# Second mixture of experts with a written-out order on TensorE, and S5 states split by real and imaginary part over partition halves

## The chip, the cores and the metric

The kernel runs on one core of one Trainium2 chip. The time is the device time of one execution in microseconds (us); lower is better. The core's engines work side by side: PE (TensorE: matmuls; PEld is its weight load), DVE (VectorE), ACT (ScalarE), POOL (GpSimd), and SP, which here issues the DMA transfers. Each takes its instructions in a fixed order and waits where an operand is late.

## The reference

Two layers over 256 latent and 256 context tokens of width 1024. A layer runs four token mixers (windowed attention, a state-space scan, global attention, S5), merges them, and then a mixture of 32 experts, two per token. The first layer works on all 512 tokens, the second on the 256 latent ones. The parts that matter here:

```python
def s5_mixer(...):
    for direction in range(2):
        a_bar, b_bar = s5_discretise(...)
        s_l, _ = s5_scan(einsum('blgs,gns->blgn', ul, b_bar), a_bar, fin_c, rev)
        y_l = y_l + real(einsum('blgn,gsn->blgs', s_l, c_cplx))
def expert_dispatch(h, expert_idx, gate_w, w_gate, w_up, w_down):
    ...
    def expert_block(args):
        xb, e = args
        return (silu(xb @ w_gate[e]) * (xb @ w_up[e])) @ w_down[e]
    y = lax.map(expert_block, (x_blocks, block_expert))
    return zeros_like(h).at[slot_tok].add(y * slot_w[:, None])
```

S5 states are complex: a real and an imaginary part of 64 states for each of 32 channel groups. An expert has three weight matrices, gate and up of 1024x512 and down of 512x1024, 2 MB each in float32.

## The kernel before, in words

The program is one Python function per stage; a framework keeps the tiles and semaphores, and its scheduler puts each engine's instructions into an order by a simulated timeline (line 1972). `tc.issue_after(x)` pins what is written inside it behind instruction x on the same engine; without it the order on an engine is the scheduler's.

**The second mixture** (layer 1, `l == 1`) has 256 tokens in two tiles (`nt` = 2) and goes through all 32 experts. The weights of an expert come as six loads of 1 MB (`load`, L1655, tile `mraw`; gate, up, down in halves), all issued by SP in program order into a ring of 16 slots; a slot comes free when the matmuls that read it are done. For an expert e, with the tile names that the profile prints:

- `front1` (L1753): `sl`, a one-hot matrix of 128 tokens by 128 slots for each token tile (two comparisons on DVE, L1757); `slb`, its first 64 slots in bf16 (L1759); 48 bf16 matmuls that gather the expert's tokens into `px` (L1764), copied by ACT into `xgt`; two transposes of `sl` into `pst` (L1770) and two products of `sl` with the router weights that give one weight per slot in a column of `pst` (L1772); DVE copies `slt` (L1774) and `wcol` (L1776) out of it. The one-hot side of expert e is made while e-1 is worked on (`nxt`).
- `product` (L1687): gate and up, 16 matmuls each (L1694), into the two halves of `pgu`. Each is two matmul records in the profile.
- `swiglu` (L1668): `th` by tanh on ACT (L1670), then two steps on DVE (printed as L84).
- `down` (L1697): two transposes of `th` into `pat` (L1701), a copy `at` on ACT, eight products into `pd` (L1707).
- `expert1` (L1779): `yg` = `pd` x `wcol` x gate (two on DVE, L84), split into `yh` (ACT) and `yl` (DVE); eight products `po` (L1800) scatter them back, four for each token tile, and DVE adds each into `acc` (L1806, printed as L78).

Where PE takes up each of these pieces is the scheduler's choice. The first mixture (layer 0, `front0`, `expert0`) uses the same `product`, `swiglu` and `down`, with gathers and scatters by DMA.

**S5** (L785 to L873) works through four blocks q of eight channel groups in each layer. Per block it loads the tables `gt`, `W`, `R`, `Q` (1 MB, L806) and `M`; for both directions d it makes `pE` on PE, runs the scan on DVE, and writes the states to `SB` (L853 to L856). `SB` holds for each d, part r (real, imaginary) and a (4 pairs of groups) a block-diagonal matrix of 128 x 128: group h in rows and columns 64h to 64h+63, zero elsewhere (cleared once, L793). The outputs `pY` come from `M` (L860, weights of 64 columns for one group h) and from `SB` (L863, weights of 128 columns for both groups, one product per d and r).

## Time and profile before

| | |
|---|---|
| median of 3 runs | 2624.61 us (2623.95 to 2629.16) |
| the profiled execution | 2621.41 us |
| its span, first to last instruction | 2619.6 us |
| granted TensorE clock, mean | 0.934 |
| PE busy | 2246.3 us, 86% |
| DVE, ACT, POOL busy | 53%, 27%, 27% |
| second mixture, first to last `swiglu` | 2099.8 to 2591.0 us |
| S5 output products L863, layer 0 and layer 1 | 378.2 to 528.0 and 1753.0 to 1834.6 us |

The time of an execution is its span and some 2 us around it. A busy PE is not a PE at its peak: matmuls are pipelined, so the time that a piece of PE work takes is best read from the start of one row to the start of the next. The profile's names leave buffer numbers out, and its "x32" counts records, two for a float32 matmul and one for a bf16 matmul.

### The profile page before, as it was taken

To read this page: it belongs to the slowest core of one execution; us is meant where nothing else is said; L and a number is where in the kernel's file an instruction comes from. 1 tells how busy PE (TensorE), PEld (TensorE's weight loads), DVE (VectorE), ACT (ScalarE), POOL (GpSimd) and SP (SyncE) were. 2 spreads that over 40 slices of the span, in tenths; PEclk is the share of its full clock that TensorE was granted. 3 is DMA by queue.
4 is the path that set the end of the run, shared out by engine and by line. 5 is a ranking of instruction groups with operands and counts; after the bars stand their busy time and mean duration, and the time that the engine had idled before them with its cause. 6 is when DMAs were issued, how large, how long until landed. Compare 5 with 4: busy or idle time off the path is not lost. (4 is left out here: it accounts for less than half of the span.)

```text
span 2619.6 us, 41026 instructions
## 1 busy us (share of the span) xinstructions
PE 2246.3 (86%) x16006; PEld 1579.7 (60%) x16006; DVE 1379.4 (53%) x2755; ACT 695.9 (27%) x1344; POOL 716.4 (27%) x686
## 2 busy tenths in 40 slices
PE   5898987799996979988888749989888699999996
PEld 3677866577654755544444338878767566755553
DVE  7846888956753852000000286558587744443334
ACT  2334422145561201111111123533465211111110
POOL 8988787743120031111111032001132100000000
PEclk8999998899997979999999869999898799999998
DMA  6643476575765779999999955488656699999991
GB/s 244 183 137 122 136 198 206 167 247 182 238 195 159 253 271 372 415 409 415 412 410 411 373 175 154 147 251 266 227 175 178 264 364 421 422 423 403 369 387 71
DMA packets 287317, 710.67 MB, mean 271 GB/s; under 512 B 39886, under 2 KB 199038, under 8 KB 228240
## 3 DMA queue, kind: packets, MB, share of 16 engines
q1 hardware_dynamic: 280400, 694.72, 73.0%
q0 software_dynamic: 5280, 8.05, 1.0%
q10 hardware_dynamic: 1440, 5.24, 0.5%
q8 instruction: 128, 2.10, 0.3%
q14 instruction: 69, 0.57, 0.1%
HBM read 645.82 MB, written 71.37 MB: 274 GB/s over the span
## 5 line engine op out<-in xcount | busy, mean ns | idle before, releaser
L1694 PE MATMUL pgu<-mraw,xgt 128*64 128x256 f32 x4224 | 515.2, 386 | 29.1 <-DMA mraw<-in_moe_w_up_dram 28.0
L1694 PEld LDWEIGHTS pgu<-mraw,xgt 128*64 128x64 f32 x4224 | 314.1, 138 | 213.6 <-DMA mraw<-in_moe_w_up_dram 58.4
L84 DVE SCALAR_TENSOR_TENSOR th<-th,pgu 128x256 f32<-128x256 f32 x132 | 55.5, 420 | 498.6 <-ACT th L1670 496.5
L1707 PE MATMUL pd<-mraw,at 128*64 128x512 f32 x1056 | 258.8, 605 | 38.9 <-DMA mraw<-in_moe_w_down_dram 36.8
L507 PE MATMUL pfm<-hhi,hi 128*128 128x256 f32 (+1 forms) x832 | 283.0, 344 | 5.3 <-ACT hi L93 4.6
L508 PE MATMUL pfm<-hlo,hi 128*128 128x256 f32 (+1 forms) x832 | 283.7, 343 | 2.1 <-DVE hlo L78 2.0
L509 PE MATMUL pfm<-hhi,lo 128*128 128x256 f32 (+1 forms) x832 | 280.9, 342 | 4.0 <-DVE lo L78 3.7
L78 DVE TENSOR_TENSOR lo<-raw,hi 128x1024 fp32r<-128x1024 f32 (+1 forms) x147 | 205.5, 1399 | 93.6 <-ACT hi L93 89.2
L128 POOL TENSOR_TENSOR bnrs<-bnrs,mhalf 128x1 f32<-128x1 f32 x26 | 28.9, 1116 | 723.3 <-DVE bnrs L88 723.3
L93 ACT ACTIVATE hi<-raw 128x1024 fp32r<-128x1024 f32 (+1 forms) x160 | 169.2, 1059 | 204.2 <-PE pfm L508 124.7
L1707 PEld LDWEIGHTS pd<-mraw,at 128*64 128x64 f32 x1056 | 80.7, 137 | 164.3 <-issue 108.4
L507 PEld LDWEIGHTS pfm<-hhi,hi 128*128 128x128 f32 x832 | 158.4, 192 | 32.8 <-ACT hi L93 6.0
L509 PEld LDWEIGHTS pfm<-hhi,lo 128*128 128x128 f32 x832 | 157.8, 191 | 24.6 <-DVE lo L78 4.6
L508 PEld LDWEIGHTS pfm<-hlo,hi 128*128 128x128 f32 x832 | 158.9, 191 | 19.7 <-DVE hlo L78 2.9
L84 DVE SCALAR_TENSOR_TENSOR yg<-pd,wcol,g 64x512 f32<-64x512 f32 x64 | 48.0, 750 | 148.0 <-PE pd L1707 135.0
L1745 POOL DMA_INDIRECT yb_d<-ye,idx x30 | 29.9, 998 | 294.2 <-ACT ye L93 266.8
L507 PE MATMUL pm<-yh,hi 128*128 128x512 f32 (+1 forms) x256 | 90.6, 368 | 21.3 <-ACT yh L93 11.9
L78 DVE TENSOR_TENSOR acc<-acc,po 128x512 f32<-128x512 f32 x124 | 80.6, 684 | 51.9 <-PE po L1800 51.3
L508 PE MATMUL pm<-yl,hi 128*128 128x512 f32 (+1 forms) x256 | 92.3, 362 | 3.4 <-DVE yl L78 3.4
L1670 ACT ACTIVATE th<-pgu 128x256 f32<-128x256 f32 x66 | 25.3, 383 | 261.4 <-PE pgu L1694 261.4
L507 PE MATMUL ptm<-hi,hhi 128*128 128x256 f32 x320 | 92.4, 289 | 0.0
L508 PE MATMUL ptm<-lo,hhi 128*128 128x256 f32 x320 | 91.3, 286 | 0.0
(508 smaller groups left out, 4470.0 us busy)
## 6 DMA issues: line engine op xcount, KB each, us to landing
mraw<-in_moe_w_gate_dram SPq DMA_DIRECT2D x132, 1024.0 KB
mraw<-in_moe_w_up_dram SPq DMA_DIRECT2D x132, 1024.0 KB
mraw<-in_moe_w_down_dram SPq DMA_DIRECT2D x132, 1024.0 KB
raw<-in_w_in_dram SPq DMA_DIRECT2D x116, 512.0 KB
modr<-in_mod_w_dram SPq DMA_DIRECT2D x40, 1024.0 KB
modw<-in_mod_w_dram SPq DMA_DIRECT2D x8, 1024.0 KB
gt_d<-gt SPq DMA_DIRECT2D x16, 512.0 KB
q_d<-Q SPq DMA_DIRECT2D x32, 256.0 KB
```

Source lines behind the costliest of these rows:

```text
L78: V.tensor_tensor(o, a, b, op=op)
L84: V.scalar_tensor_tensor(o, a, s, b, op0=op0, op1=op1)
L93: S.activation(o, a, AF.Copy, scale=scale)
L128: G.tensor_tensor(o, a, b, op=OP.pow)
L507: T.matmul(p, ahi, bhi, start=first, stop=False)
L508: T.matmul(p, ahi, blo, start=False, stop=False)
L509: T.matmul(p, alo, bhi, start=False, stop=last)
L1670: S.activation(th, pg, AF.Tanh, scale=0.5)
L1694: T.matmul(p[64 * cb:64 * cb + 64, 256 * i:256 * i + 256], xt[:, kt], raw[:, k, 256 * cb:256 * cb + 256], start=(kt == 0), stop=(kt == KT ...
L1707: T.matmul(p[64 * nh:64 * nh + 64], at[:, j, 64 * cb:64 * cb + 64], raws[cb][:, j, nh], start=(k == 0), stop=(k == 3))
L1745: sc_ = G.indirect_dma_start(out=yb_d.rearrange("r (n c) -> (r n) c", n=2), out_offset=bass.IndirectOffsetOnAxis(ap=i, axis=0), in_=y, in_ ...
```

## The change

**The second mixture** gets a loop of its own, `experts1`, and its PE work is pinned piece behind piece. `in_order()` opens `issue_after` behind the last instruction kept in `behind`; it does nothing in layer 0, where `behind` stays empty. For expert e PE now takes: the gather of e+1 (`px`), the transposes `pst` of e+1, the scatter of expert e-2 for token tile 1, up of e, gate of e+1, the transposes `pat` of e, the scatter of expert e-1 for token tile 0, down of e. The loads follow this order: up of e, gate of e+1, down of e. `slb` is compared into bf16 directly; `slw`, in place of `sl`, is the comparison times the router weight; `slt` is the transposed `slw` compared with zero; `wcol` is its row sum on DVE, and the products of L1772 are gone. `slt` has four buffers. `route_over` (the list of overfull experts) is written at expert 3 instead of 2.

**S5**: `SB` keeps the real part in partitions 0 to 63 and the imaginary part in 64 to 127, for each d, h and a a matrix of 128 x 64 with no zeros. The products of L863 become one per d and h with 64 weight columns into the half of `pY` for h; their count is the same. `Q` is read by two transfers of 64 partitions each.

```diff
@@ -789,7 +789,8 @@
-            SB = s1.tile([128, 2, 2, 4, 128], F32, name="SB")
+            SB = s1.tile([128, 2, 2, 4, 64], F32, name="SB")
             V.memset(SB, 0.0)
...
@@ -803,7 +804,8 @@
                     Q = sq.tile([128, 2, 2, 4, 128], F32, tag="Q", name="Ql", bufs=1)
-                    dma(Q, q_d[l, q])
+                    for r in range(2):
+                        dma(Q[64 * r:64 * r + 64], q_d[l, q].rearrange("(h s) d r a x -> r s d h a x", h=2)[r])
...
@@ -846,7 +848,7 @@
                         for h in range(2):
                             hp = slice(64 * h, 64 * h + 64)
                             for r in range(2):
-                                o0 = SB[hp, d, r, :, 64 * h:64 * h + 64]
+                                o0 = SB[64 * r:64 * r + 64, d, h]
                                 i1, i2 = (m1[hp, 0], m2[hp, 1]) if r == 0 else (m1[hp, 1], m2[hp, 0])
...
@@ -859,9 +861,8 @@
                         for h in range(2):
                             T.matmul(py[64 * h:64 * h + 64, a], U[:, grp(a, h)], M[:, 2 * a + h], start=True, stop=False)
                         for d in range(2):
-                            for r in range(2):
-                                T.matmul(py[:, a], SB[:, d, r, a], Q[:, d, r, a], start=False,
-                                         stop=(d == 1 and r == 1))
+                            for h in range(2):
+                                T.matmul(py[64 * h:64 * h + 64, a], SB[:, d, h, a], Q[:, d, h, a], start=False, stop=(d == 1))
...
@@ -1684,6 +1685,17 @@
+        behind = [None]
+
+        @contextmanager
+        def in_order():
+            if behind[0] is None:
+                yield
+            else:
+                with tc.issue_after(behind[0].ins):
+                    yield
+
         def product(p, i, e, xt):
 
...
-                        T.matmul(p[64 * cb:64 * cb + 64, 256 * i:256 * i + 256], xt[:, kt],
-                                 raw[:, k, 256 * cb:256 * cb + 256], start=(kt == 0), stop=(kt == KT - 1))
-
-        def down(p, e, a):
+                        o = T.matmul(p[64 * cb:64 * cb + 64, 256 * i:256 * i + 256], xt[:, kt],
+                                     raw[:, k, 256 * cb:256 * cb + 256], start=(kt == 0), stop=(kt == KT - 1))
+            return o
+
+        def down(p, e, a, between=None):
             at = wk.tile([128, 2, 128], F32, tag="at", name="at2")
             pt = pb("pat")
-            for j in range(2):
-                T.transpose(pt[:, 128 * j:128 * j + 128], a.rearrange("q (p j) -> q j p", j=2)[:, j], ident)
+            with in_order():
+                for j in range(2):
+                    o = T.transpose(pt[:, 128 * j:128 * j + 128], a.rearrange("q (p j) -> q j p", j=2)[:, j], ident)
             copyS(at.rearrange("p a b -> p (a b)"), pt[:, :256])
+            if l:
+                behind[0] = o
+            if between:
+                between()
             raws = [load(rows_of(2, e, 256 * cb, 256)).rearrange("p (j n) c -> p j n c", j=2) for cb in range(2)]
-            for k in range(4):
-                cb, j = divmod(k, 2)
-                for nh in range(2):
-                    T.matmul(p[64 * nh:64 * nh + 64], at[:, j, 64 * cb:64 * cb + 64], raws[cb][:, j, nh],
-                             start=(k == 0), stop=(k == 3))
+            with in_order():
+                for k in range(4):
+                    cb, j = divmod(k, 2)
+                    for nh in range(2):
+                        o = T.matmul(p[64 * nh:64 * nh + 64], at[:, j, 64 * cb:64 * cb + 64], raws[cb][:, j, nh],
+                                     start=(k == 0), stop=(k == 3))
+            if l:
+                behind[0] = o
 
...
         def front1(e):
 
-            sl = wk.tile([128, nt, 128], F32, tag="sl", name="sl")
+            slb = wk.tile([128, nt, 64], BF16, tag="slb", name="slb")
+            slw = wk.tile([128, nt, 128], F32, tag="sl", name="slw")
             for t in range(nt):
-                ts(sl[:, t], slots[:, 1], rt["posx"][:, t, e:e + 1], None, OP.is_equal)
-            slb = wk.tile([128, nt, 64], BF16, tag="slb", name="slb")
-            V.tensor_copy(slb, sl[:, :, :64])
+                ts(slb[:, t], slots[:, 1, :64], rt["posx"][:, t, e:e + 1], None, OP.is_equal)
+            for t in range(nt):
+                ts(slw[:, t], slots[:, 1], rt["posx"][:, t, e:e + 1], rt["wx"][:, t, e:e + 1], OP.is_equal, OP.mult)
             px = pb("px")
-            for kt in range(KT):
+            pst = pb("pst")
+            with in_order():
+                for kt in range(KT):
+                    for t in range(nt):
+                        for i in range(3):
+                            T.matmul(px[:, 64 * kt:64 * kt + 64], rt["h2"][t][i][:, 128 * kt:128 * kt + 128], slb[:, t],
+                                     start=(t == 0 and i == 0), stop=(t == nt - 1 and i == 2))
                 for t in range(nt):
-                    for i in range(3):
-                        T.matmul(px[:, 64 * kt:64 * kt + 64], rt["h2"][t][i][:, 128 * kt:128 * kt + 128], slb[:, t],
-                                 start=(t == 0 and i == 0), stop=(t == nt - 1 and i == 2))
+                    behind[0] = T.transpose(pst[:, 128 * t:128 * t + 128], slw[:, t], ident)
             xt = wk.tile([128, KT, 64], F32, tag="xt", name="xgt")
             copyS(xt.rearrange("p a x -> p (a x)"), px)
-            pst = pb("pst")
-            for t in range(nt):
-                T.transpose(pst[:, 128 * t:128 * t + 128], sl[:, t], ident)
-            for t in range(nt):
-                T.matmul(pst[:, 256:257], sl[:, t], rt["wx"][:, t, e:e + 1], start=(t == 0), stop=(t == nt - 1))
-            slt = wk.tile([128, nt, 128], F32R, tag="slt", name="slt")
-            V.tensor_copy(slt.rearrange("p a x -> p (a x)"), pst[:, :128 * nt])
+
+            slt = wk.tile([128, nt, 128], F32R, tag="slt", name="slt", bufs=4)
+            ts(slt.rearrange("p a x -> p (a x)"), pst[:, :128 * nt], 0.0, None, OP.is_gt)
             wcol = wk.tile([128, 1], F32, tag="wcol", name="wcol")
-            V.tensor_copy(wcol, pst[:, 256:257])
+            V.tensor_reduce(wcol, pst[:, :128 * nt], axis=AXL.X, op=OP.add)
             return xt, slt, wcol
 
-        def expert1(e, xt, slt, wcol, nxt):
...
+        def gate1(e, xt):
+            p = pa("pgu")
+            with in_order():
+                behind[0] = product(p, 0, e, xt)
+            return p
+
+        def scatter1(t, e, yh, yl, slt):
+            for t in (t,):
                 po = [pc("po") for _ in range(2)]
+                with in_order():
+                    for i, yy in enumerate((yh, yl)):
+                        for nh in range(2):
+                            hs = slice(64 * nh, 64 * nh + 64)
+                            behind[0] = T.matmul(po[nh], slt[hs, t], yy[hs], start=(i == 0), stop=(i == 1))
...
-        front, expert = ((front0, expert0), (front1, expert1))[l]
+
+        def experts1():
+            f = front1(0)
+            pgu = gate1(0, f[0])
+            done = late = None
+            for e in range(32):
+                if e == 3:
+                    route_over(rt, wk)
+                xt, slt, wcol = f
+                f = front1(e + 1) if e < 31 else None
+                if late:
+                    scatter1(1, *late)
+                with in_order():
+                    behind[0] = product(pgu, 1, e, xt)
+                a = swiglu(pgu[:, :256], pgu[:, 256:], 256)
+                if f:
+                    pgu = gate1(e + 1, f[0])
+                p = pm_("pd")
+                down(p, e, a, (lambda: scatter1(0, *done)) if done else None)
+                late = done
+                yh = wk.tile([128, 512], F32R, tag="yh", name="yh")
+                yl = wk.tile([128, 512], F32R, tag="yl", name="yl")
+                yg = wk.tile([128, 512], F32, tag="yg", name="yg")
+                for nh in range(2):
+                    hs = slice(64 * nh, 64 * nh + 64)
+                    stt(yg[hs], p[hs], wcol[hs], g2[1][hs, 512 * nh:512 * nh + 512], OP.mult, OP.mult)
+                copyS(yh, yg)
+                tt(yl, yg, yh, OP.subtract)
+                done = e, yh, yl, slt
+            scatter1(1, *late)
+            for t in range(nt):
+                scatter1(t, *done)
+
...
-        f = start0(0) if l == 0 else front(0)
+        if l == 1:
+            experts1()
+        else:
+            f = start0(0)
...
```

The order on PE, the second mixture, a late expert, before (the two products of L1772 for the next expert, half of `pd`, then `pgu` of the next expert with the scatter `po` between its parts, and `pat`):

```order
L1772 MATMUL pst<-oh_17684,sl 128x1 x2
L1707 MATMUL pd<-mraw,at_22186 64x512 x4
L1694 MATMUL pgu<-mraw,xgt 64x256 x16
L1800 MATMUL po<-yh,slt 128x512 x2
L1800 MATMUL po<-yl,slt 128x512 x2
L1694 MATMUL pgu<-mraw,xgt 64x256 x8
L1800 MATMUL po<-yh,slt 128x512
L1800 MATMUL po<-yl,slt 128x512
L1800 MATMUL po<-yh,slt 128x512
L1800 MATMUL po<-yl,slt 128x512
L1694 MATMUL pgu<-mraw,xgt 64x256 x8
L1701 MATMUL pat<-identr,th 128x128 x2
```

And before, an early expert:

```order
L1770 MATMUL pst<-identr,sl 128x128 x2
L1772 MATMUL pst<-oh_17684,sl 128x1 x2
L1701 MATMUL pat<-identr,th 128x128 x2
L1800 MATMUL po<-yh,slt 128x512
L1800 MATMUL po<-yl,slt 128x512
L1800 MATMUL po<-yh,slt 128x512
L1800 MATMUL po<-yl,slt 128x512
L1694 MATMUL pgu<-mraw,xgt 64x256 x11
L1707 MATMUL pd<-mraw,at_20223 64x512 x8
L1694 MATMUL pgu<-mraw,xgt 64x256 x5
```

The change, every expert after the first ones (the last row begins the 48 gather products, L1788, of the next expert):

```order
L1791 MATMUL pst<-identr,slw 128x128 x2
L1814 MATMUL po<-yh,slt 128x512 x2
L1814 MATMUL po<-yl,slt 128x512 x2
L1706 MATMUL pgu<-mraw,xgt 64x256 x32
L1715 MATMUL pat<-identr,th 128x128 x2
L1814 MATMUL po<-yh,slt 128x512 x2
L1814 MATMUL po<-yl,slt 128x512 x2
L1726 MATMUL pd<-mraw,at_22171 64x512 x8
L1788 LDWEIGHTS hb_0_17800
```

What moved: before, `pat` stands directly behind `pgu` late in the stage, and behind the gather early in it; now there are always the sixteen products of the next expert's gate between the up products of an expert and its `pat` (the 32 `pgu` products of one row are up of e and gate of e+1), the scatter stands in two places, and the two products of L1772 are gone.

The order on DVE, one expert of the second mixture, before:

```order
L84 SCALAR_TENSOR_TENSOR th<-th,pgu 128x256 x2
L88 TENSOR_SCALAR sl<-k_slots,oh_17683 128x128 x2
L1759 CAST slb<-sl 128x128
L84 SCALAR_TENSOR_TENSOR yg<-pd,wcol,g_18060 64x512 x2
L78 TENSOR_TENSOR yl<-yg,yh 128x512
L78 TENSOR_TENSOR acc_18058<-acc_18058,po 128x512 x2
L78 TENSOR_TENSOR acc_18059<-acc_18059,po 128x512 x2
L1774 CAST slt<-pst 128x256
L1776 COPY wcol<-pst 128x1
```

The change:

```order
L84 SCALAR_TENSOR_TENSOR yg<-pd,wcol,g_18068 64x512 x2
L88 TENSOR_SCALAR slb<-k_slots,oh_17691 128x64 x2
L88 TENSOR_SCALAR slt<-pst 128x256
L1798 TENSOR_REDUCE wcol<-pst 128x1
L90 TENSOR_SCALAR slw<-k_slots,oh_17691,oh_17692 128x128 x2
L78 TENSOR_TENSOR acc_18067<-acc_18067,po 128x512 x2
L78 TENSOR_TENSOR yl<-yg,yh 128x512
L84 SCALAR_TENSOR_TENSOR th<-th,pgu 128x256 x2
L78 TENSOR_TENSOR acc_18066<-acc_18066,po 128x512 x2
```

What moved: `slb` is made without `sl`, `slw` behind `slt` and `wcol` of the expert before it; the additions into `acc` stand in two places, ahead of `yl` and behind `th`.

The order on PE in S5, layer 0, before and then the change:

```order
L860 MATMUL pY<-Ml,U 64x128 x2
L863 MATMUL pY<-Ql,SB 128x128 x4
L860 MATMUL pY<-Ml,U 64x128 x2
L863 MATMUL pY<-Ql,SB 128x128 x4
L407 MATMUL pst<-Q,BD 32x128
L860 MATMUL pY<-Ml,U 64x128 x2
L863 MATMUL pY<-Ql,SB 128x128 x4
```

```order
L862 MATMUL pY<-Ml,U 64x128 x2
L865 MATMUL pY<-Ql,SB 64x128 x4
L862 MATMUL pY<-Ml,U 64x128 x2
L865 MATMUL pY<-Ql,SB 64x128 x4
L862 MATMUL pY<-Ml,U 64x128 x2
L865 MATMUL pY<-Ql,SB 64x128 x3
L407 MATMUL pst<-Q,BD 32x128
L865 MATMUL pY<-Ql,SB 64x128
```

What moved: nothing in the count of products; those of `SB` have 64 weight columns in place of 128 (L865).

## Rows read from the trace of the kernel before

**Rows 1.** The page: the span, and each engine's busy time and instructions

```profile
span 2619.6 us, 41026 instructions
...
PE 2246.3 (86%) x16006; PEld 1579.7 (60%) x16006; DVE 1379.4 (53%) x2755; ACT 695.9 (27%) x1344; POOL 716.4 (27%) x686
```

**Rows 2.** One line, L1670 (opens `swiglu`): second mixture, then a stretch of the first

```profile
L1670 ACT ACTIVATE th<-pgu x32: 383/383/385, 2099.8 to 2591.0; 128x256 f32<-128x256 f32 x32
...
L1670 ACT ACTIVATE th<-pgu x14: 383/383/384, 1099.1 to 1307.0; 128x256 f32<-128x256 f32 x14
```

**Rows 3.** Stretches: early expert, late expert, first mixture, S5 of layer 1, second mixture's begin

```profile
core 0: us, PE busy (x) PEld busy (x) DVE busy (x) ACT busy (x) POOL busy (x), PEclk, DMA share, GB/s
...
2200.00:2214.70 14.70, 14.70 (x148) 10.25 (x146) 6.64 (x14) 2.00 (x5) 0.00 (x0) 1.00 1.01 419
2444.01:2460.29 16.28, 14.88 (x144) 8.47 (x144) 6.64 (x14) 2.00 (x4) 0.00 (x0) 1.00 0.91 342
...
1100.00:1200.00 100.00, 81.15 (x573) 42.84 (x574) 5.39 (x13) 13.29 (x26) 12.77 (x13) 1.00 1.02 408
...
1730.00:1800.00 70.00, 58.16 (x636) 51.95 (x636) 45.69 (x96) 19.42 (x31) 4.89 (x2) 0.90 1.00 310
...
2120.00:2140.00 20.00, 20.00 (x173) 13.09 (x171) 8.72 (x21) 2.00 (x4) 0.00 (x0) 1.00 0.84 282
```

**Rows 4.** Waits, 2120 to 2604: who waited, for whom, us, times, longest

```profile
PE pat L1701 <- DVE th L84: 21.1, 15, 1.5
```

**Rows 5.** Timeline of a late expert: start, length, engine, line, count, idle before

```profile
2444.01 0.38 ACT L1670 ACTIVATE th<-pgu 128x256 f32<-128x256 f32 x1 [8.91 <-PE pgu L1694]
...
2445.36 0.51 PE L1701 MATMUL pat<-identr,th 128*128 128x128 f32 x2 [1.39 <-DVE th L84]
...
2445.71 1.30 PE L1764 MATMUL px<-slb,hb 128*128 128x64 bf16 x39
...
2446.94 3.65 PE L1707 MATMUL pd<-mraw,at 128*64 128x512 f32 x16
...
2450.80 0.41 PE L1770 MATMUL pst<-identr,sl 128*128 128x128 f32 x2
...
2451.05 0.51 PE L1772 MATMUL pst<-oh,sl 128*128 128x1 f32 x4
...
2451.48 3.67 PE L1694 MATMUL pgu<-mraw,xgt 128*64 128x256 f32 x32
...
2455.09 0.50 PE L1800 MATMUL po<-yh,slt 64*128 64x512 f32 x2
...
2455.75 1.95 PE L1694 MATMUL pgu<-mraw,xgt 128*64 128x256 f32 x16
```

**Rows 6.** Groups by line on DVE, 2120 to 2604: busy, mean ns

```profile
L1774 DVE CAST slt<-pst 128x256 fp32r<-128x256 f32 x29 | 12.1, 418 | 0.0
...
L1446 DVE TENSOR_REDUCE ovt<-bcm 128x16 f32<-128x512 f32 x1 | 0.7, 687 | 0.0
```

**Rows 7.** DMA, 2140 to 2320

```profile
DMA packets 10415, 75.98 MB, mean 422 GB/s; under 512 B 1155, under 2 KB 1155, under 8 KB 1155
```

**Rows 8.** Timeline of SP, loads as the second mixture begins

```profile
2087.27 0.33 SPq L1655 DMA_DIRECT2D mraw<-in_moe_w_up_dram  x1
2094.59 2.05 SPq L1655 DMA_DIRECT2D mraw<-in_moe_w_down_dram  x2
```

**Rows 9.** Timeline of PE, S5 of layer 1

```profile
1813.24 0.44 PE L860 MATMUL pY<-Ml,U 128*64 128x128 f32 x4
1813.61 1.16 PE L863 MATMUL pY<-Ql,SB 128*128 128x128 f32 x8
1814.70 0.44 PE L860 MATMUL pY<-Ml,U 128*64 128x128 f32 x4
```

**Rows 10.** Waits in 360 to 560, S5 of layer 0

```profile
PE pY L863 <- DVE SB L78: 23.2, 7, 7.5
```

**Rows 11.** Tile `Ql`: its transfers

```profile
L806 SPq DMA_DIRECT2D Ql<-q_d x8: 347/414/455, 350.9 to 1789.3; - x8
```

More of the change, by code (lines that the diff above doesn't have):

```diff
@@ L1 @@
 import math
-from contextlib import ExitStack
+from contextlib import ExitStack, contextmanager
 import numpy as np
@@ L1775, in front1 @@
             wcol = wk.tile([128, 1], F32, tag="wcol", name="wcol")
-            V.tensor_copy(wcol, pst[:, 256:257])
+            V.tensor_reduce(wcol, pst[:, :128 * nt], axis=AXL.X, op=OP.add)
             return xt, slt, wcol
-        def expert1(e, xt, slt, wcol, nxt):
-            pgu = pa("pgu")
-            for i in range(2):
-                product(pgu, i, e, xt)
-            front = nxt()
-            a = swiglu(pgu[:, :256], pgu[:, 256:], 256)
-            p = pm_("pd")
-            down(p, e, a)
-            yh = wk.tile([128, 512], F32R, tag="yh", name="yh")
-            yl = wk.tile([128, 512], F32R, tag="yl", name="yl")
-            yg = wk.tile([128, 512], F32, tag="yg", name="yg")
-            for nh in range(2):
-                hs = slice(64 * nh, 64 * nh + 64)
-                stt(yg[hs], p[hs], wcol[hs], g2[1][hs, 512 * nh:512 * nh + 512], OP.mult, OP.mult)
-            copyS(yh, yg)
-            tt(yl, yg, yh, OP.subtract)
-            for t in range(nt):
-                po = [pc("po") for _ in range(2)]
-                for i, yy in enumerate((yh, yl)):
-                    for nh in range(2):
-                        hs = slice(64 * nh, 64 * nh + 64)
-                        T.matmul(po[nh], slt[hs, t], yy[hs], start=(i == 0), stop=(i == 1))
@@ L1806, in expert1 @@
                         tt(o, o, po[nh], OP.add)
-            return front
-        front, expert = ((front0, expert0), (front1, expert1))[l]
+        def experts1():
[29 more added lines that the diff above has]
+                scatter1(t, *done)
         g2 = {}
@@ L1812, in moe @@
             g2[1] = mod_bc(bc, l, 5, 1, "g21")
-        f = start0(0) if l == 0 else front(0)
+        if l == 1:
+            experts1()
+        else:
+            f = start0(0)
         order = list(range(20)) + [32 + b for b in range(SPARE[l])] + list(range(20, 32)) + [None]
-        for e, n in zip(order[:-3], order[1:]):
+        for e, n in zip(order[:-3], order[1:]) if l == 0 else ():
             if e == 2:
                 route_over(rt, wk)
-            f = expert(e, *f, lambda: front(n) if l else (n, *front(n)))
+            f = expert0(e, *f, lambda: (n, *front0(n)))
         if l == 0:
@@ L1834, in moe @@
                     ts(slt[:, i, t], slots[:, 0], off[:, t, i:i + 1], None, OP.is_equal)
-        f = expert(30, *f, lambda: front(31) if l else (31, *front(31)))
-        expert(31, *f, lambda: None)
+            f = expert0(30, *f, lambda: (31, *front0(31)))
+            expert0(31, *f, lambda: None)
         with tc.issue_after(rt["load"].ins):
```

## The prediction

> **What bounds the kernel now.** I read the page first: PE is busy 86% of a span of 2619.6 us, DVE 53% [rows 1]. Such a share is a mean over stages, so each part of the change has to be priced in its own stage.
>
> For the second mixture I took one line that runs once per expert, L1670. Its 32 starts reach from 2099.8 to 2591.0 us [rows 2]: 31 periods in 491.2 us, 15.85 us each. The windows show two kinds of period [rows 3]. The early one, 14.70 us, is all PE: 14.70 busy, DMA share 1.01. The late one, 16.28 us, has PE busy for 14.88, and DMA moves less, 342 against 419 GB/s, because slots come free later. The list of waits says what PE waits for: 15 times for `th`, 21.1 us in all, up to 1.5 each [rows 4]. The timeline shows the place: `th` starts on ACT at 2444.01, when the last `pgu` product is done, and `pat` starts at 2445.36 after 1.39 us of idle PE [rows 5]. The order on PE says why: late in the stage `pat` stands directly behind `pgu`, early in it the gather lies between. So PE bounds the stage, with a stall that the order makes.
>
> **The change, part by part.**
>
> *The period without stall.* From start to start in the timeline [rows 5], with records counted: the gather (39 of its 48 records in 2446.94 - 2445.71 = 1.23, so 1.51 for all), `pst` 0.25, the products of L1772 0.43, the `pgu` products (32 of 64 records in 2455.09 - 2451.48 = 3.61, so 7.22), the scatter of one token tile 0.66, so 1.32 for two, `pat` 0.35, and 3.6 for `pd`, whose row of 3.65 overlaps the next a little. The sum is 14.7, the early period of [rows 3]. So nothing is left unexplained, and PE can do no expert faster than these pieces.
>
> *What goes.* The products of L1772: 0.43 us of PE per expert, which leaves 14.3.
>
> *What moves.* Between `swiglu`'s start and `pat` PE now has the gate of the next expert, 3.6 us. The chain that it must cover took 2445.36 - 2444.01 = 1.35 us [rows 5]: covered, with 2 us to spare. Between `pat` and `pd` stands a scatter of 0.66; what it covers is the copy `at`. Between the gather and the gate that reads `xgt` stand `pst`, a scatter and the up products, 4.5 us. The scatters use results one and two experts old. So I take no stall: 14.3.
>
> *DVE, which now must keep pace.* It was busy 6.64 us of a period [rows 3]. New are a comparison out of PSUM (128x256), a row sum (128x256) and `slw`; two casts and a copy go. The nearest rows are the cast it replaces, 0.42, and a sum over twice as many elements, 0.69 [rows 6]. Below, the new ones cost what the old did; above, the row sum costs 0.69 where the copy cost little, and DVE comes to some 7.5 of 14.3. I take that upper value and cost it at nothing: PE is the cover, and in DVE's new order `slb` stands a whole expert ahead of the gather that reads it. `route_over`, a few sums like that of [rows 6], moves one expert later on the same half idle engine: nothing.
>
> *The loads.* Gate of e+1 is now asked for before down of e, the order in which PE uses them. The stream moved 75.98 MB in 180 us, 422 GB/s [rows 7]; a load is 128 x 2048 x 4 bytes, 1.049 MB: 2.48 us a load, 14.9 us an expert. That is more than 14.3, so the lead of the loads shrinks, and it has to last. The sixteenth of the 192 loads was issued at 2087.27, the next two at 2094.59 [rows 8]; 176 from there on at 2.48 end at about 2531. From 2120 to 2140 the stream ran at 282 GB/s [rows 3], a loss of 20 x (1 - 282/422) = 7 us, so 2538. PE at 14.3 per expert begins the last `pd` at about 2099.8 + 2 + 31 x 14.3 + 1.4 = 2546 (2 for the second gather, which now precedes the first up). The slack is near 8 us: the loads stay hidden, but only just.
>
> *Sum of the mixture.* 31 x 14.3 = 443.3 against 491.2: 47.9 us less. A scatter or two missing in the first experts and the 2 us at the start cancel. I take 47. Behind the last `swiglu` the steps are the same ones.
>
> *S5.* A pair of groups takes four records of L860 in 0.37 us and eight of L863 in 1.09 [rows 9]: 0.093 and 0.136 a record. With 64 weight columns on halves of the output, as L860 has them, the eight cost 0.74: 0.35 saved, 16 times a layer, 5.6 us. In layer 0 PE waits for `SB` there, 23.2 us [rows 10], so nothing is gained. In layer 1 it counts where PE is the bound. Against it: `Q` in two issues, each 0.41 us on SP [rows 11], in a stretch where DMA is fully busy at 310 GB/s, against 419 with large rows [rows 3]. If splitting brings `Q` from the one rate to the other, its 1.05 MB take 0.9 us longer: 3.6 a layer. Writes of `SB` whose output lies on other partitions than the input appear nowhere in this trace; equal cost is my value, since the writes keep count and size. Gain below 6, loss below 5; I take 4 us less, as most of the products lie behind the DMA-bound stretch. Clearing half the `SB` is short on DVE, once a layer: nothing.
>
> The Trainium skill ("DMA: Bandwidth & Descriptors", Rules for kernel authors) speaks against this part: transfers to disjoint partition halves serialize, so use one over 128 partitions. By it the split gains nothing and costs an issue; no run here shows the two halves, and the sum has only the loss above. The skill also says ("TensorEngine Tiling (Array Packing)", Theoretical Speedup) that 64 columns allow up to twice the rate. The trace disagrees in size, 0.093 to 0.136 or 1.5 times; by the rule layer 1 would gain 8.7 in place of 5.6, and the total would be 3 lower.
>
> *The rest.* The scheduler lays out the other stages anew around these edits; DVE and PE in the mixers change order in small ways, such as one `pY` product moved. I cost it at nothing, with 10 us either way.
>
> **Sum.** 2621.4 - 47 - 4 = 2570 for a profiled execution; the median of the runs stands 3.2 above that execution. So **2574 us**.
>
> **Rivals.**
>
> *The loads become the bound.* For: the slack above is 8 us, and in the first mixture 13 periods took 1307.0 - 1099.1 = 207.9 us, 16.0 each [rows 2], with PE busy 81% and DMA at 1.02 and 408 GB/s [rows 3]. Against: that stream also carries gathers, and 180 us here ran at 422. At 16.0 us for six loads, 176 loads take 469: to 2564 and, with the same 7, 2571, and the second half of the last `pd` to 2573. Before, it ended near 2597 (2591.0, the chain of 1.35, `pat`, the copy, 3.6). So 24 less, and S5's 4: 2621.4 - 28 + 3.2 = 2597. Chance 0.09.
>
> *Part of a stall stays.* With PE pinned, each late operand stops all of it: `at` behind a scatter of 0.66, `xgt`, a buffer of `po`. 0.5 us an expert gives 15.5 back: 2590. Chance 0.14. Mixers that lose some 15 in the new layout give the same time: 0.07.
>
> *Slower.* `pat` waits for `th` again, now because of DVE: `th` stands in its fixed order behind `yg` of the expert before, `slt`, the row sum, `slw`, two additions into `acc` and `yl`, and `yg` begins only when `pd` of that expert ends. From there to the need for `th` PE has 1.5 + 0.25 + 0.66 + 7.2 = 9.6 us of work. If DVE needs longer, PE stops for the remainder in every expert. It decides at 15.85 - 14.3 = 1.55 us, so with a chain of 11.2; at 12 the period is 16.7, the stage 518, 26 more, and with S5's 4 the kernel 2647. Against: DVE's whole work for an expert is 7.5 by the rows above, and it would have to be half as much again. Chance 0.04.
>
> That the pins do not hold is excluded by the order on PE, where each expert reads as the one before.
>
> **How the numbers follow.** 0.66 for the forecast, with 2556 to 2588 from its bounds (0.2 us an expert is 6 us; S5 -2 to +9; mixers 10 either way), 0.09, 0.14, 0.07 and 0.04 for the others. The range takes in the rivals at 2590 and the one at 2597: **2552 to 2600**. A measurement of this kernel tells about 0.2%, 5 us, from no change: faster 0.94, within it 0.02, slower 0.04.
>
> **What would show it.** Right: L1670 at even steps of 14.2 to 14.5 us from the fourth expert to the last; no wait of `pat` for `th`; PE 100% busy in the mixture; DMA at 1.0 until shortly before its end, SP waiting for `pgu` and `pd`. S5: rows of the new L865 start 0.09 apart in layer 1, while in layer 0 the wait for `SB` stays or grows. Wrong: `pgu` or `pd` waiting for `mraw` near the end (first rival), a wait of PE repeated once per expert (second, third), or stages ahead of 1700 us that begin over 10 us earlier or later.

## The result and the profile after

| | before | after |
|---|---|---|
| median of 4 runs | 2624.28 us (2623.28 to 2629.16) | 2580.88 us (2574.12 to 2584.93) |
| the profiled execution's span | 2619.6 us | 2572.2 us |
| from the first `swiglu` of the second mixture to the last | 491.2 us | 441.8 us |
| last modulation product of layer 0 | 814.6 us | 825.0 us |

The ratio is 0.9832, interval 0.9814 to 0.9849: 43 us faster. The line that opens `swiglu` (now L1671) shows in which stages; its tile's source view, first mixture and second mixture, of the kernel after:

```profile
L1671 ACT ACTIVATE th<-pgu x34: 375/383/384, 984.3 to 1497.1; 128x256 f32<-128x256 f32 x34
...
L1671 ACT ACTIVATE th<-pgu x32: 383/384/386, 2103.3 to 2545.1; 128x256 f32<-128x256 f32 x32
```

and the first mixture of the kernel before:

```profile
L1670 ACT ACTIVATE th<-pgu x34: 375/383/385, 974.8 to 1487.3; 128x256 f32<-128x256 f32 x34
```

Against these and [rows 2]: the mixers of layer 0 end 9.5 us later (984.3 - 974.8), the first mixture keeps its 512 us, the stretch from its last `swiglu` to the first of the second takes 606.2 in place of 612.5, the second mixture 441.8 in place of 491.2, and what is left after it 27.1 in place of 28.6. Together 9.5 + 0.3 - 6.3 - 49.4 - 1.5 = -47.4, the difference of the spans. The -6.3 of the stretch between the mixtures is within what executions of one kernel differ: in the repetition below that stretch takes 610.1.

Over the whole second mixture PE's idle time shrinks, and its work too; one window each, before and after, with the columns of [rows 3]:

```profile
2099.80:2591.00 491.20, 468.81 (x4452) 289.88 (x4449) 207.99 (x441) 61.63 (x124) 0.00 (x0) 1.00 0.93 376
```

```profile
2103.30:2545.10 441.80, 439.14 (x4286) 247.40 (x4282) 218.15 (x460) 57.95 (x124) 0.00 (x0) 1.00 1.00 415
```

Idle time falls from 22.4 to 2.7 us, and most of what went were the waits of [rows 4]. PE's work falls by 29.7 us. Of this the products of L1772 are 31 x 0.34 to 0.43, 11 to 13 us. The other 17 to 19 us are time that PE before took longer for the same pieces, late in the stage above all; no run here takes that apart.

In an expert from the fourth to the 26th PE is never idle; the window of one of them:

```profile
2200.00:2214.17 14.17, 14.17 (x143) 8.07 (x140) 7.11 (x17) 1.88 (x4) 0.00 (x0) 1.00 1.01 417
```

Its timeline, with the expert's pieces, which answers to [rows 5]:

```profile
2205.54 0.51 PE L1715 MATMUL pat<-identr,th 128*128 128x128 f32 x2
2205.98 0.50 PE L1814 MATMUL po<-yh,slt 64*128 64x512 f32 x2
...
2206.64 3.65 PE L1726 MATMUL pd<-mraw,at 128*64 128x512 f32 x16
2210.23 1.57 PE L1788 MATMUL px<-slb,hb 128*128 128x64 bf16 x48
...
2211.64 0.42 PE L1791 MATMUL pst<-identr,slw 128*128 128x128 f32 x2
2211.99 0.50 PE L1814 MATMUL po<-yh,slt 64*128 64x512 f32 x2
...
2212.65 7.13 PE L1706 MATMUL pgu<-mraw,xgt 128*64 128x256 f32 x64
2216.37 0.38 ACT L1671 ACTIVATE th<-pgu 128x256 f32<-128x256 f32 x1 [3.08 <-PE pgu L1706]
...
2219.71 0.50 PE L1715 MATMUL pat<-identr,th 128*128 128x128 f32 x2
```

No PE row has an idle time. `th` starts at 2216.37 in the middle of the 64 `pgu` records, and `pat` comes 3.34 us later without waiting. From start to start the pieces are 0.44, 0.66, 3.59, 1.41, 0.35, 0.66 and 7.06: 14.17. From the 27th expert on this changes. The line of `th` from there, and the timeline of one such expert:

```profile
L1671 ACT ACTIVATE th<-pgu x4: 383/384/386, 2471.4 to 2516.3; 128x256 f32<-128x256 f32 x4
```

```profile
2486.34 0.38 ACT L1671 ACTIVATE th<-pgu 128x256 f32<-128x256 f32 x1 [3.35 <-PE pgu L1706]
...
2488.36 1.49 PEld L1706 LDWEIGHTS pgu<-mraw,xgt 128*64 128x64 f32 x16 [0.79 <-DMA mraw<-in_moe_w_gate_dram]
2488.36 1.95 PE L1706 MATMUL pgu<-mraw,xgt 128*64 128x256 f32 x16 [0.34 <-DMA mraw<-in_moe_w_gate_dram]
2493.34 0.20 PEld L1726 LDWEIGHTS pd<-mraw,at 128*64 128x64 f32 x4 [0.95 <-DMA mraw<-in_moe_w_down_dram]
```

Three periods in 44.9 us, 14.97 each, or 2.50 us a load: here the loads are the bound. Over the longer stretch DMA moved 416 GB/s, with the columns of [rows 3], so 2.52 us for a load of 1.049 MB:

```profile
2120.00:2530.00 410.00, 408.85 (x4028) 231.32 (x4028) 207.16 (x438) 54.26 (x115) 0.00 (x0) 1.00 1.00 416
```

### The profile page after: what moved, and what is told of

It reads as the page before. It is cut to its first block, busy times and chain, and to the rows that moved or that the text cites. A ratio compares the mean times of both kernels' runs of the same rounds, so it can differ in the third digit from the quotient of the medians.

```text
span 2572.2 us, 40839 instructions
## 1 busy us (share of the span) xinstructions
PE 2199.5 (86%) x15878; PEld 1514.0 (59%) x15878; DVE 1403.1 (55%) x2787; ACT 692.3 (27%) x1344; POOL 724.5 (28%) x686
## 5 line engine op out<-in xcount | busy, mean ns | idle before, releaser
L1706 PE MATMUL pgu<-mraw,xgt 128*64 128x256 f32 x4224 | 494.4, 385 | 30.1 <-DMA mraw<-in_moe_w_up_dram 27.0
L1706 PEld LDWEIGHTS pgu<-mraw,xgt 128*64 128x64 f32 x4224 | 298.7, 138 | 220.2 <-DMA mraw<-in_moe_w_up_dram 57.5
L1726 PE MATMUL pd<-mraw,at 128*64 128x512 f32 x1056 | 251.7, 604 | 39.9 <-DMA mraw<-in_moe_w_down_dram 38.0
L1726 PEld LDWEIGHTS pd<-mraw,at 128*64 128x64 f32 x1056 | 72.2, 136 | 182.1 <-issue 112.7
L78 DVE TENSOR_TENSOR acc<-acc,po 128x512 f32<-128x512 f32 x124 | 79.6, 683 | 99.7 <-PE po L1814 99.6
L164 PE MATMUL pm<-modr,cond 128*32 128x512 f32 x320 | 61.2, 684 | 38.4 <-DMA modr<-in_mod_w_dram 38.3
L509 PE MATMUL ptm<-hi,hlo 128*128 128x256 f32 x320 | 91.7, 287 | 0.0
```

The costliest lines, as they stand in the source:

```text
L78: V.tensor_tensor(o, a, b, op=op)
L164: T.matmul(pm[32 * (j0 + j):32 * (j0 + j) + 32, :], cond[:, kt, :], w[:, j * 512:(j + 1) * 512], start=(kt == 0), stop=(kt == KT - 1))
L509: T.matmul(p, alo, bhi, start=False, stop=last)
L1706: o = T.matmul(p[64 * cb:64 * cb + 64, 256 * i:256 * i + 256], xt[:, kt], raw[:, k, 256 * cb:256 * cb + 256], start=(kt == 0), stop=(kt == ...
L1726: o = T.matmul(p[64 * nh:64 * nh + 64], at[:, j, 64 * cb:64 * cb + 64], raws[cb][:, j, nh], start=(k == 0), stop=(k == 3))
```

## The experiments

All are timed against the kernel before on the same chip. The S5 part and the mixture part can be had apart: taking one of them back leaves the other's PE order as it was.

**The parts alone.** Mixture only: the four hunks of S5 taken back. S5 only: these four put into the kernel before. A third keeps the old S5 in layer 0:

```diff
-            SB = s1.tile([128, 2, 2, 4, 64], F32, name="SB")
+            SB = s1.tile([128, 2, 2, 4, 64] if l else [128, 2, 2, 4, 128], F32, name="SB")
...
-                    for r in range(2):
+                    if l == 0:
+                        dma(Q, q_d[l, q])
+                    for r in range(2) if l else ():
...
```

> The new mixture with the S5 of before. Theory: the two parts add, and all of the gain is the mixture's. Its first swiglu starts at about 2100 us as before, 26 periods are 14.2 us, the last few 15.0, so the profile ends some 50 us before that of the kernel before: span about 2569 to 2572. Rival (the S5 part carries some of the gain, because the mixture starts with other loads ahead of it): the gain stays under 44 us.

> The new S5 with the mixture of before. Theory: layer 0 loses 9 to 10 us behind S5 (the modulation loads modr end later), layer 1 gains 6, so the kernel is 2 to 5 us slower than before, with the first swiglu of the second mixture near 2103. Rival (the 10 us of layer 0 belong to one profiled execution, not to the order): about 10 us faster than before, since S5 itself ends 13 us earlier in layer 0 and 6 in layer 1.

> The whole change, with the S5 of before kept in layer 0 alone. Theory: layer 0 returns to the order of before and its 9.5 us come back, so the span is 2562 to 2566 and this is the fastest of the three. Rival (layer 0's loss is not the order of the modulation loads): within 4 us of the changed kernel, near 2572.

> The changed kernel once more, to see where its runs of 2574 to 2585 us differ. Theory: the mixture is near the rate of its loads, so a slower execution has more waits for mraw there and periods of 15 us earlier than the 27th expert; all stages ahead of it agree within 3 us. Rival: the mixers of layer 0 or 1 vary, and the mixture keeps 442 us.

| | median, us | ratio to before, interval | first `swiglu`, first mixture | second mixture |
|---|---|---|---|---|
| mixture only | 2571.8 | 0.9815 (0.9792 to 0.9839) | 974.5 | 441.4 |
| S5 only | 2642.5 | 1.0082 (1.0060 to 1.0104) | 984.4 | 503.7 |
| new S5 in layer 1 alone | 2568.0 | 0.9800 (0.9776 to 0.9823) | 978.2 | 442.3 |
| the change again | 2581.1 | 0.9844 (0.9817 to 0.9871) | 989.1 | 440.6 |

The whole gain is the mixture's, 51 us alone. The S5 part takes 9 of them back, in layer 0: of the kernels up to here and the three of the pins and the slot weights below, those that have it there begin the first mixture at 982 to 989 us, the others at 974 to 978. Alone it costs 20, more than I expected, since the mixture without pins also came out in another order behind it, with periods up to 19.9 us; so the two parts do not add up to the 43 of the whole. New S5 in layer 1 alone (2568.0) can't be told from none (2571.8), as their intervals overlap. The repetition went against the theory that its executions differ by waits for loads: the mixture kept 441 us, and the mixers took longer, 5 us in layer 0 and 4 in layer 1.

**Where layer 0 loses.** S5 itself ends early there, its last `ysb` at 515.1 in place of 528.4. But behind it, from 561 us on, 24 loads of 1 MB for the modulation pass through one buffer (`modr`, L162), four products each (`pm`, L164). PE's timeline of these products, and SP's of the loads, of the kernel after:

```profile
585.42 1.04 PE L164 MATMUL pm<-modr,cond 128*32 128x512 f32 x2
...
611.62 1.05 PE L164 MATMUL pm<-modr,cond 128*32 128x512 f32 x2
...
628.40 1.04 PE L164 MATMUL pm<-modr,cond 128*32 128x512 f32 x2
```

```profile
561.25 0.93 SPq L162 DMA_DIRECT2D modr<-in_mod_w_dram  x1
...
629.48 0.33 SPq L162 DMA_DIRECT2D modr<-in_mod_w_dram  x1
```

and SP's of the kernel before:

```profile
567.57 0.33 SPq L162 DMA_DIRECT2D modr<-in_mod_w_dram  x1
...
579.49 0.33 SPq L162 DMA_DIRECT2D modr<-in_mod_w_dram  x1
...
598.79 0.33 SPq L162 DMA_DIRECT2D modr<-in_mod_w_dram  x1
...
640.05 0.38 SPq L162 DMA_DIRECT2D modr<-in_mod_w_dram  x1
```

In its new layout the scheduler spread the products of the first load over 43 us, from 585.42 on, and the second load could go out only at 629.48; in the kernel before, two more had gone out by then. There the third load held the buffer as long, from 598.79 to 640.05, so the buffer costs time in that kernel as well. After, the chain of loads ends with the product at 825.0, and the merge stands behind it. A window of the kernel after, in that wait:

```profile
800.00:820.00 20.00, 5.80 (x24) 0.60 (x24) 0.00 (x0) 0.00 (x0) 0.00 (x0) 0.50 0.42 152
```

PE is busy for 5.8 of 20 us at a granted clock of 0.5, its lower level of 1.2 GHz, after 38 of the 40 us from 740 to 780 at 1.00 and 12.9 of the next 20 at 0.85; DVE, ACT and POOL do nothing. So I let PE take these products as soon as the load is there:

```diff
-                for j in range(n):
-                    T.matmul(pm[32 * (j0 + j):32 * (j0 + j) + 32, :], cond[:, kt, :], w[:, j * 512:(j + 1) * 512],
-                             start=(kt == 0), stop=(kt == KT - 1))
+                with tc.high_priority() if l + i and n == 4 else ExitStack():
+                    for j in range(n):
+                        T.matmul(pm[32 * (j0 + j):32 * (j0 + j) + 32, :], cond[:, kt, :], w[:, j * 512:(j + 1) * 512],
+                                 start=(kt == 0), stop=(kt == KT - 1))
```

> The changed kernel; only the four products of each modulation load in the mixers (pm from modr, 24 loads in layer 0 through one buffer) get high priority, so that PE takes them when the load lands and the buffer comes free at once. Theory (the loss of layer 0 is that buffer: in the changed kernel the first of these loads holds it from 585 to 629 us, and the merge waits behind the last one at 825): the last pm of layer 0 comes before 800, the first swiglu of the first mixture before 974 instead of 984 to 989, and the kernel is 10 to 35 us faster than the changed one. Rival (the loss is DVE's or the attention's order): first swiglu still at 980 to 990, time within 5 us of the changed kernel.

2538.2 us, ratio 0.9692 (0.9665 to 0.9720): 43 us under the change, more than the theory's 10 to 35. The same window of this kernel:

```profile
800.00:820.00 20.00, 19.68 (x86) 15.67 (x85) 15.81 (x23) 6.26 (x9) 0.00 (x0) 1.00 0.68 190
```

Its loads follow each other by some 10 us from the start, the last product of layer 0 comes at 780.5, and the first mixture begins at 943.5. So the buffer is what held layer 0: both with the new S5 in it and with the old one (below) the first mixture now begins at 939 to 945.

> The kernel with the modulation products first, and the S5 of before: what the S5 part is worth once its loss is mended. Theory (S5's lead of 13 us in layer 0 was eaten only by the modulation buffer): first swiglu of the first mixture some 8 to 13 us later than the 943.5 of the kernel with both, the kernel 8 to 16 us slower than it. Rival (S5 lies beside other work in both layers): first swiglu within 4 us of 943.5, the time within 5 us.

> The kernel before with nothing but the priority for the modulation products. Theory (the single buffer of these loads sets the end of layer 0's mixers in every version): the last pm before 790 instead of 814, the first swiglu of the first mixture at 945 to 955 instead of 975, and with the mixtures as before 20 to 30 us faster. Rival (it only mends what the S5 part broke): under 6 us faster.

> The modulation products first, the new mixture, and the new S5 in layer 1 alone. Theory (S5 is beside other work in both layers once the modulation buffer is mended): within 5 us of the kernel with the S5 of before, 2527 to 2537 us, first swiglu of the first mixture at 938 to 945. Rival (in layer 1 the shorter products count): 4 to 8 us faster than that kernel, with the stretch from the last swiglu of the first mixture to the first of the second at 597 us or less in place of 603.

On the kernel before, the priority alone gives 2591.7 us, 0.9880 (0.9865 to 0.9896): 30 us, with the first mixture at 941.2; again the mixture without pins came out longer, 504.1 us. With the new mixture and the old S5 it gives 2532.4, **0.9665** (0.9649 to 0.9681), the fastest measured, with the first mixture at 939.3; with the new S5 in layer 1 alone 2536.4, 0.9679 (0.9652 to 0.9706). The intervals overlap with those of the kernel with both: the new S5 brings nothing that these runs can tell, in either layer. The expected 8 to 16 us did not come: with the old S5 the kernel was, if anything, 6 us faster. S5's earlier end lies beside other work.

**What the pins and the place of gate do.** No pins: `in_order` made to do nothing. Gate late:

```diff
-                if f:
-                    pgu = gate1(e + 1, f[0])
                 p = pm_("pd")
                 down(p, e, a, (lambda: scatter1(0, *done)) if done else None)
+                if f:
+                    pgu = gate1(e + 1, f[0])
```

> The changed kernel with the same program order of the second mixture but without pinning on PE. Theory (the pins keep the order that covers the chain from swiglu to pat): periods of 14.2 us as long as the scheduler keeps the order as written, some two thirds of the experts, then 15 to 16.5 with waits of pat for th; mixture 10 to 25 us longer than 442. Rival (the order as written is enough): all periods 14.2 but the last few, within 4 us of the changed kernel.

> The changed kernel with gate of e+1 placed behind down of e, all still pinned: same work, but nothing between up of e and its pat. Theory: PE waits 1.35 to 1.5 us for th in every expert, periods near 15.6, mixture about 484 us, the kernel 35 to 45 us slower than the changed one, so about as slow as before. Rival (the gain is the missing products and the loads, not the cover): periods at most 14.6, under 13 us slower.

Gate late: 2629.0 us, 1.0030 (1.0018 to 1.0043), 48 above the change, a little over the 35 to 45 expected, and no faster than before. Periods are 15.7 us, the mixture takes 487.8. Its timeline, and its waits in the mixture:

```profile
2258.85 0.38 ACT L1671 ACTIVATE th<-pgu 128x256 f32<-128x256 f32 x1 [3.87 <-PE pgu L1706]
2260.28 0.48 PE L1715 MATMUL pat<-identr,th 128*128 128x128 f32 x2 [1.48 <-DVE th L84]
```

```profile
PE pat L1715 <- DVE th L84: 47.4, 32, 1.5
```

The wait of [rows 4] is back in every expert, 1.48 us each, 47.4 us in all. No pins: 2602.0 us, 0.9936 (0.9911 to 0.9960), 21 above the change. The size is the theory's, the wait is another. Its periods are 14.2 us up to the 12th expert and 15.6 from the 15th on, and there its timeline says:

```profile
2409.43 0.50 PE L1814 MATMUL po<-yh,slt 64*128 64x512 f32 x2 [0.61 <-ACT yh L93]
2410.15 0.50 PE L1814 MATMUL po<-yl,slt 64*128 64x512 f32 x2 [0.22 <-DVE yl L78]
...
2415.01 0.51 PE L1715 MATMUL pat<-identr,th 128*128 128x128 f32 x2
```

The scheduler put the scatter too close behind its own expert's `pd`, 0.83 us of waiting, and `pat` doesn't wait. The other 0.6 us of the period I did not take apart; PE's rows there are shorter runs of mixed kinds.

**The slot weights by products again.**

```diff
+            for t in range(nt):
+                ts(slo[:, t], slots[:, 1], rt["posx"][:, t, e:e + 1], None, OP.is_equal)
...
+                for t in range(nt):
+                    behind[0] = T.matmul(pst[:, 256:257], slo[:, t], rt["wx"][:, t, e:e + 1], start=(t == 0), stop=(t == nt - 1))
...
-            V.tensor_reduce(wcol, pst[:, :128 * nt], axis=AXL.X, op=OP.add)
+            V.tensor_copy(wcol, pst[:, 256:257])
```

> The changed kernel with the slot weights made again by two products on PE (and the plain one-hot for them by two comparisons more on DVE). Theory: 0.43 us of PE in every expert, periods of 14.6, 10 to 13 us slower. Rival (the products hide among weight loads, so the row sum brought nothing): periods stay at 14.2.

The source view of its L1671, and that of the kernel after, both from 2150 to 2450:

```profile
L1671 ACT ACTIVATE th<-pgu x21: 385/385/386, 2150.1 to 2440.2; 128x256 f32<-128x256 f32 x21
```

```profile
L1671 ACT ACTIVATE th<-pgu x21: 383/384/384, 2159.7 to 2443.0; 128x256 f32<-128x256 f32 x21
```

20 periods take 290.1 in place of 283.3: the products cost 0.34 us an expert. But the kernel takes 2583.0 (0.9867, 0.9838 to 0.9895), not measurably more than the change. At 14.5 us no expert waits for its loads, so the mixture takes only 5.6 us more, 447.4 in place of 441.8, and the spread of the mixers hides them.

**Why the products of `pY` became so short.** In the kernel with the modulation first, PE's timeline in S5 of layer 1 shows the twelve records of a pair of groups, from the first row of six records to the next:

```profile
1819.07 0.59 PE L866 MATMUL pY<-Ql,SB 128*64 128x128 f32 x6
1819.39 0.27 PE L863 MATMUL pY<-Ml,U 128*64 128x128 f32 x1
1819.49 0.27 PE L866 MATMUL pY<-Ql,SB 128*64 128x128 f32 x1
1819.50 0.38 PE L863 MATMUL pY<-Ml,U 128*64 128x128 f32 x2
1819.61 0.27 PE L866 MATMUL pY<-Ql,SB 128*64 128x128 f32 x1
1819.71 0.27 PE L863 MATMUL pY<-Ml,U 128*64 128x128 f32 x1
1819.72 0.59 PE L866 MATMUL pY<-Ql,SB 128*64 128x128 f32 x6
```

Twelve records in 0.65 us, 0.055 each; before, the twelve of [rows 9] took 1.46, and I forecast 1.11. To see whether the halves run side by side, the products were written group by group:

```diff
                         for h in range(2):
                             T.matmul(py[64 * h:64 * h + 64, a], U[:, grp(a, h)], M[:, 2 * a + h], start=True, stop=False)
-                        for d in range(2):
-                            for h in range(2):
+                            for d in range(2):
                                 T.matmul(py[64 * h:64 * h + 64, a], SB[:, d, h, a], Q[:, d, h, a], start=False, stop=(d == 1))
```

> The kernel with the modulation products first, with the six products of pY for a pair of groups written group by group, so that neighbours write the same half of the output columns instead of halves in turn. Theory (products on the two halves run side by side, which is why a pair's twelve records take 0.66 us and not the 1.11 that I forecast): 1.1 us or more for twelve records where they stand together. Rival (64 weight columns alone make them short): still 0.66.

```profile
1815.76 0.44 PE L865 MATMUL pY<-Ql,SB 128*64 128x128 f32 x4
1815.97 0.27 PE L863 MATMUL pY<-Ml,U 128*64 128x128 f32 x1
1816.03 0.27 PE L865 MATMUL pY<-Ql,SB 128*64 128x128 f32 x1
1816.08 0.27 PE L863 MATMUL pY<-Ml,U 128*64 128x128 f32 x1
1816.14 0.33 PE L865 MATMUL pY<-Ql,SB 128*64 128x128 f32 x2
1816.25 0.27 PE L863 MATMUL pY<-Ml,U 128*64 128x128 f32 x1
1816.30 0.27 PE L865 MATMUL pY<-Ql,SB 128*64 128x128 f32 x1
1816.36 0.27 PE L863 MATMUL pY<-Ml,U 128*64 128x128 f32 x1
1816.41 0.44 PE L865 MATMUL pY<-Ql,SB 128*64 128x128 f32 x4
```

Again 0.65, the number of the rival. But the run, a single execution of 2535.4 us, doesn't decide between the two, for the edit did not part the halves in time. The two records of a product of L863 stand at 1815.97 and 1816.08, and those of the next at 1816.25 and 1816.36: 0.11 apart each time, with a record of L865 between them. PE went through two sequences at once here too.

Other rows speak for the theory. The eight records of L863 in [rows 9] stand unbroken by others; without the first of them their row reads

```profile
1813.83 0.94 PE L863 MATMUL pY<-Ql,SB 128*128 128x128 f32 x7
```

with 0.27 us for the last record, so six steps in 0.67 us, 0.112 each. In the kernel after, the last two records of S5 in layer 1, behind which no other product of `pY` comes, are

```profile
1845.62 0.38 PE L865 MATMUL pY<-Ql,SB 128*64 128x128 f32 x2
```

again 0.11 apart. So a record of 64 columns that comes alone is no shorter than one of 128. What is new is that two start together: 1819.49 and 1819.50, then 1819.71 and 1819.72 above, a pair every 0.11 us, which is 0.055 a record. That the two lie on different halves is inferred from the program; the profile does not print the half. The rest of the 1.46 us of [rows 9] stood where the width changes: four records of L860 took 0.37, though as two pairs they need 0.22, and the eight of L863 took 1.09, though unbroken they need 0.89. That is 0.35 us for the two changes between 64 and 128 columns.

## Why the prediction was right, and where it was not

- *The period, 14.3 without stall.* 14.17. The sum over pieces held; unbroken `pgu` took 7.06 in place of 7.22.
- *No stall, the gate covers the chain.* Shown by the late gate, which brought 1.48 us an expert back, 48 us in all: this is what the cover is worth in the new order. It is not its share of the gain, since before only 15 experts waited for `th`, 21.1 us [rows 4]. Of the 49 us that the stage won, some 20 are idle time and 30 are shorter work of PE. The prediction named the stall and the products of L1772, and not the rest of the 30; its total came out all the same, as it is the measured 491.2 less 31 periods of the new order.
- *The products of L1772, 0.43.* 0.34 by their return, and of the 31 x 0.34 = 10.5 us only 5.6 in the mixture, as the loads bound its end without them.
- *DVE at 7.5.* 7.11 busy of 14.17, no wait of PE for it but once, 1.5 us in the last expert, which has no next gate to cover the chain; the rival that was slower did not come.
- *The loads, hidden but only just.* The rate was nearly right, 2.48 forecast and 2.50 to 2.52 measured, the slack wasn't. The step that set 2538 against 2546 left out that PE would be faster still, 31 x 0.13 = 4 us, and 176 loads slower by 0.04 are 7 more. Against these, its loss of 7 us at the begin is not seen again, so the terms do not make up the whole slack, and the rest stays open. From the 27th expert PE's weight load waits for `mraw`, periods are up to 0.8 longer, some 3 us in all. The first rival came true at the end of the stage, at about an eighth of its price of 23.
- *S5, 4 us less.* Here the working failed, in three terms. "0.093 a record" was read from four records of L860 in [rows 9] that are two pairs with a change of width behind them, and 0.136 holds a change too; unbroken, the steps are 0.055 and 0.112. What the Trainium skill says ("TensorEngine Tiling (Array Packing)", Theoretical Speedup), up to twice the rate, agrees with this trace, 0.112 to 0.055; that the trace disagrees, as the prediction says, was a misreading. Where its records stand together a pair of groups saved 0.81 us in place of 0.35, up to 13 us of PE in a layer. But it had no effect in layer 1, where the stretch from clearing `SB` to the last `ysb` took 99.2 us after 99.7. In layer 0, where I expected nothing, S5 ended 13 us earlier in the first profile, and all of it and 10 more went to the modulation buffer; why it ended earlier was not taken apart.
- *"The rest ... I cost it at nothing, with 10 us either way."* This was the step that was off: the S5 part costs 9 us in the median, through the order of the modulation products in layer 0. With it at nothing and S5 at -4, as forecast, the total came out at 2574; without S5 the forecast of the mixture, 2578, has 2571.8 beside it. That the total, 2581, lies only 7 us off was luck in part: the mixture gave 51 for 47, and S5 took 9 for a gain of 4. The bound 2588 does not follow from its terms, either; 9 and 10 above 2574 are 2593.
- *`Q` in two transfers.* Each issue took SP 0.62 us in place of 0.41 [rows 11], so 1.24 for 0.41 a load, by the tile's view after:

```profile
L808 SPq DMA_DIRECT2D Ql<-q_d x16: 579/620/1647, 351.1 to 1805.2; - x16
```

What the halves do to the DMA queues was not tried by itself, so no run here shows whether they serialize, as the Trainium skill says ("DMA: Bandwidth & Descriptors", Rules for kernel authors).

## What to carry to other kernels

Cover a chain between engines by work of the next step, pin it, and check the cover by taking it away: here that is worth 1.5 us in each of 32 steps, and the pinned stage kept its 440 to 442 us behind every change of the other stages, while the free one moved between 491 and 504. Where a scheduler orders the rest, an edit that saves time in one stage has to be followed to the next wait: a buffer that is held by products taken one by one cost more than the edit saved, and one line of priority on them gave 30 us to the kernel before and 43 to the changed one. When a stage gets faster, work out again when its last load lands.

## What the runs showed of the hardware that I had not expected

A float32 record over 128 x 128 data came every 0.11 us with 128 weight columns (before), and with 64 columns two came at a time, a pair every 0.11 us (modulation first); alone, one of 64 columns took its 0.11 as well (after). The two changes of width in a pair of groups cost 0.35 us [rows 9]. PE kept a granted clock of 1.00, its upper level of 2.4 GHz, through the whole mixture, where it was busy for 439 of 442 us; it had 0.50, the lower level, in the stretch of layer 0 where it was busy for 5.8 of 20 us.
